# Third pair's left sums in the second chunk, spills of x in SyncE's queue, and the down projection's first two groups by half columns: one decoder layer on one Trainium2 core

## The chip, the cores and the metric

The kernel runs on one NeuronCore of a Trainium2 chip. The metric is the device time of one execution in microseconds (us); the time of a kernel is the median of several runs. A core has these engines: TensorE (PE: matmuls and transposes; its loads of the stationary operand are shown apart as PEld), VectorE (DVE), ScalarE (ACT), GpSimd (POOL) and SyncE (SP, which only issues DMAs). ACT and POOL can issue DMAs too. Every engine works through its own instructions in the order of the program; semaphores tie the engines together. Matmuls write to PSUM, eight banks of 128 x 512 float32; everything else lies in SBUF.

## The reference

One decoder layer on 256 tokens of width 2048, all float32 with random weights:

```python
h = rmsnorm(x, norm_attn_pre);  proj = h @ w_in
mixed = concat(dilated_window_attention(...), latent_attention(...))     # 8 + 8 heads
x = x + rmsnorm(mixed @ w_out, norm_attn_post)
h = rmsnorm(x, norm_mlp_pre)
u = square(relu(h @ w_up))              # 2048 -> 8192
x = x + rmsnorm(u @ w_down, norm_mlp_post)   # 8192 -> 2048
```

The change touches the second half: from the residual after `w_out` through the up projection to the first columns of the down projection.

## The kernel before

**Precision and weights.** The product of two float32 matrices is made of three matmuls of a faster type: each operand is split into a high and a low part (`hi` = the value rounded, made by ACT; `lo` = value less `hi`, made by DVE), and hi*hi, hi*lo and lo*hi are summed in PSUM (function `three`, or the loop in `down_mm`). So every weight tile of 128 x 1024 goes through four stages: a DMA into a `raw` tile (5 buffers, issued by SP at L169), `hi` on ACT (L268, or L272 where a gain is multiplied in), `lo` on DVE (L269 or L273), and the matmuls (L258). `hi` and `lo` have 8 buffers each. Class `Weights` holds a list of all weight tiles in the order of their use; `get(i)` emits the load and split of all tiles up to `i + 1 + ahead`, with `ahead` 6 (4 around the norm). Load and split of a tile are emitted together, but SP runs ahead of ACT as far as free `raw` tiles allow.

**Order of the rest.** The instructions are emitted by hand in one order per engine. A class `Flow` keeps a clock that counts the planned time of the emitted matmuls and transposes. Work beside the matmuls (evacuation of PSUM, norms, sums) is written as generators: each `yield t` says that the rest is to be emitted when the clock has advanced by `t` us; `flow.pump()` is called after each group of matmuls, `flow.finish(chain)` emits a chain to its end at once.

**Residual.** For each of the two blocks of 128 tokens, `residual(b)` updates `xs[b]` on DVE (L750, four quarters), transposes it on PE (`ht`), splits it into `hT` (hi and lo), and then writes `xs[b]` to DRAM as `xkeep[b]` with a DMA of 1 MB that ACT issues (L765); the squares for the next norm follow (L769). `x_back` reads `xkeep` near the end for the last residual. After both residuals the pools `po` and `mix` (with `xs` in it) are released, and the pool `up` takes their place.

**Up projection.** Eight chunks `j` of 1024 columns. In chunk 0 there are 16 single steps (128 rows of `w_up` each, 6 matmuls of 512 columns for each token block): the first 7 for block 0, then the same 7 for block 1, then the others for both blocks, 12 matmuls a step. From chunk 1 on, 10 single steps are left (five, then a wide one, two, a wide one, one, a wide one, two). The three wide steps take two row blocks and both token blocks at once and need 7 products instead of 8 (a scheme like Strassen's, in Winograd's form), so 21 matmuls instead of 24. They need sums of the weights (function `seven`: two loads `raw_w` of 512 KB, four DVE sums L321 to L324, four splits) and sums of the activations, which are the same for all chunks: `left_sums(kp)` for the three pairs `kp` = 0, 1, 2. These read and rewrite a part of `hT` (DVE L848 to L856, ACT L860, DVE L863) through two tiles `f` and `q`. The wide weights of chunks 1 to 6 are loaded by GpSimd (L316), those of chunk 7 through SP.

`all_sums` starts in chunk 0 at its ninth step and makes the three pairs one behind the other.

**Evacuation.** After chunk `j` each of its four accumulators is handled by a chain `up_evac`: for `j` > 0 a DVE addition (L819), then ACT's relu into a tile `r` (L822), then, D_UP = 1.8 us of the clock later, four transposes on PE (`rt`, in the accumulator's own bank), and ACT's square into `uT` (L830). `r`, and `f` and `q` of the left sums, share one tag with 2 buffers. The tiles `c` (function `close`, L881 and L883) hold sums of the wide products, and there are four tags of one buffer each.

**Down projection.** 16 groups `g` of 512 rows (4 steps `kk` of 128), two column halves `c` of 1024. `split_u(g)` splits the group's activations on ACT and DVE. The order is g outside, c inside. The accumulators of the half c = 1 lie in the banks of chunk 7's accumulators, so that before (g, c) = (0, 1) the chains of chunk 7 are finished.

Of the kernel before, what the change touches and what calls it, by code (L numbers as in the profile page):

```python
# [225 lines left out]
def layer(nc, tc, io):  # L226
# [79 lines left out]
    def seven(j, kp):  # L306


        st, tt, H = {}, nc.vector.tensor_tensor, 512

        def sums():
            for i, n in enumerate("ab"):
                src, name = up_weight(j, 2 * kp + i), f"raw_w{j}_{kp}{i}"
                if j < FF // CW - 1:
                    st[n] = late["up"].tile([P, CW], F32, tag="W", bufs=2, name=name)
                    nc.gpsimd.dma_start(out=st[n], in_=src)  # L316
                else:
                    st[n] = weights.load(src, CW, name)
            a, b = st["a"], st["b"]
            t, u = st["t"], st["u"] = [late["up"].tile([P, CW], F32, tag="T", bufs=2, name=f"{n}{j}_{kp}") for n in "tu"]  # L320
            tt(out=t[:, H:], in0=b[:, H:], in1=a[:, H:], op=OP.subtract)  # L321
            tt(out=u[:, :H], in0=t[:, H:], in1=a[:, :H], op=OP.add)
            tt(out=u[:, H:], in0=b[:, :H], in1=u[:, :H], op=OP.subtract)
            tt(out=t[:, :H], in0=a[:, H:], in1=a[:, :H], op=OP.subtract)  # L324

        def b11(hi, lo):
            split(hi[:, :H], lo[:, :H], st["a"][:, :H])

        return sums, [b11] + [lambda hi, lo, n=n: split(hi, lo, st[n]) for n in "but"]
# [4 lines left out]
    for j in range(FF // CW):  # L334
        wide_u.append([])
        for what, k in [("k", k) for k in range(KD)] if j == 0 else UP_STEPS:
# [5 lines left out]
                ts = [weights.plan(f) for f in fs]  # L342
                after = len(weights.specs)
            wide_u[j].append((what, k, ts))
    down = []
    for g in range(FF // 512):
        down.append({(c, kk): weights.plan(io["w_down"][(4 * g + kk) * P:(4 * g + kk + 1) * P, c * CW:(c + 1) * CW], 1, CW)
                     for c in range(2) for kk in range(4)})

    def in_order(n, apart=(0, 0)):  # L350

# [389 lines left out]
    def residual(b):  # L741

        po, yg, hT = late["po"], late["yg"], late["hT"]
        nc.vector.reduce_sum(ssr[b][:, 0:1], ssy[b], axis=mybir.AxisListType.X)
        r = rstd_of(ssr[b][:, 0:1], 1, D, f"post{b}", (pws[:, 0, b:b + 1], pws[:, 1, b:b + 1]))

        def update(ns):
            cs = [slice(n * 512, (n + 1) * 512) for n in ns]
            for c in cs:
                nc.vector.scalar_tensor_tensor(out=xs[b][:, c], in0=yg[b][:, c], scalar=r, in1=xs[b][:, c],  # L750
                                               op0=OP.mult, op1=OP.add)

        update((0, 1))
        yield D_NORM
        for n in range(4):
            t = tp_bank(f"ht{n}{b}")
            for k in range(4):
                transpose(t[:, k * P:(k + 1) * P], xs[b][:, n * 512 + k * P:n * 512 + (k + 1) * P])
            tv = t.rearrange("p (k s) -> p k s", k=4)
            if n in (0, 1):  # L760
                update((n + 2,))
            split(hT[0][:, 4 * n:4 * n + 4, b * P:(b + 1) * P], hT[1][:, 4 * n:4 * n + 4, b * P:(b + 1) * P], tv)
            parts[b] += 1
            yield D_HT
        nc.scalar.dma_start(out=xkeep[b], in_=xs[b])  # L765
        for n in range(4):
            c = slice(n * 512, (n + 1) * 512)
            junk = po.tile([P, 512], BF16, tag="junk", bufs=1, name=f"junkx{n}{b}")
            nc.scalar.activation(junk, xs[b][:, c], AF.Square, accum_out=ssx[b][:, n:n + 1])  # L769
            yield 0.5  # L770
        nc.vector.reduce_sum(ssr[b][:, 1:2], ssx[b], axis=mybir.AxisListType.X)
        rstd2[b] = rstd_of(ssr[b][:, 1:2], 1, D, f"pre2{b}", (1.0 / D, pws[:, 2, b:b + 1]))
        if b == NB - 1:
            weights.ahead = W_AHEAD
# [38 lines left out]

    def up_evac(j, b, i, acc, order, more=None):

        last = j >= 14
        yield (UP_STEP - 0.3 * last) * order
        if more is not None:
            nc.vector.tensor_tensor(out=acc, in0=acc, in1=more, op=OP.add)  # L819
            yield 0.9 if last else 1.6  # L820
        r = late["up"].tile([P, 512], F32, tag="r", bufs=2, name=f"r{j}_{b}")
        nc.scalar.activation(r, acc, AF.Relu, scale=rstd2[b])  # L822
        yield D_UP
        t = bank(i, f"rt{j}_{b}")
        for k in range(4):
            transpose(t[:, k * P:(k + 1) * P], r[:, k * P:(k + 1) * P])
        if j not in uT:
            tag = {"tag": "WT"[j // 2 - 6], "bufs": 2} if j >= 12 else {}
            uT[j] = late["up"].tile([P, CW], F32, name=f"uT{j}", **tag).rearrange("p (k s) -> p k s", k=4)
        nc.scalar.activation(uT[j][:, :, b * P:(b + 1) * P], t.rearrange("p (k s) -> p k s", k=4), AF.Square)  # L830
# [12 lines left out]
    def left_sums(kp):  # L843

        up, k, tt = late["up"], 2 * kp, nc.vector.tensor_tensor
        f, q = [up.tile([P, 512], F32, tag="r", bufs=2, name=f"{n}{kp}") for n in ("f", "q")]
        hs = [t[:, k:k + 2, :].rearrange("p k s -> p (k s)") for t in hT]
        tt(out=f, in0=hs[0].bitcast(F32), in1=hs[1].bitcast(F32), op=OP.add)  # L848
        for i in range(2):
            nc.vector.tensor_scalar_mul(f[:, i * S:(i + 1) * S], f[:, i * S:(i + 1) * S], gcol[:, 8 + k + i:9 + k + i])  # L850
        a11, a21, a12, a22 = [f[:, i * P:(i + 1) * P] for i in range(4)]
        s1, s2, s3, s4 = [q[:, i * P:(i + 1) * P] for i in range(4)]
        tt(out=s1, in0=a21, in1=a22, op=OP.add)
        tt(out=s2, in0=s1, in1=a11, op=OP.subtract)
        tt(out=s3, in0=a11, in1=a21, op=OP.subtract)
        tt(out=s4, in0=a12, in1=s2, op=OP.subtract)  # L856
        st = [up.tile([P, 512], F32R, name=f"st{kp}_{w}") for w in ("hi", "lo")]
        yield 3.0
        for t, x in ((hs, f), (st, q)):
            nc.scalar.activation(t[0], x, AF.Copy)  # L860
        yield 1.5
        for t, x in ((hs, f), (st, q)):
            tt(out=t[1], in0=x, in1=t[0].bitcast(F32), op=OP.subtract)  # L863
        sums.append([[t[:, i * P:(i + 1) * P] for t in st] for i in range(4)])
        yield 0.5

    def all_sums():
        for kp in range(N_SEVEN):
            yield from left_sums(kp)

    def three(out, a, w, first, last):

# [15 lines left out]
    for j in range(FF // CW):  # L888
# [9 lines left out]
        for t, b in order:  # L898
            what, k, tiles = steps[t]
            if (j, t, b) == (0, 8, 0):  # L900
                flow.finish(*res)
                late["po"].release()
                mix.release()
                late["up"] = pool("up", "right")
                s_chain = flow.start(all_sums())
            if (j, t, b) == (FF // CW - 1, 4, 0):
                weights.limit -= 1
                u_next = split_u(0)
# [40 lines left out]
    for i, (b, n) in enumerate(((0, 0), (0, 1), (1, 0), (1, 1))):  # L949
        y[b][n] = bank(i, f"y{b}{n}")  # L950
    ssd = [con.tile([P, 4], F32, name=f"ssd{b}") for b in range(NB)]
    GT = FF // 512

    def down_mm(u, g, kk, b, ns):

        wh, wl = weights.get(down[g][ns[0] // 2, kk])
        k = 4 * g + kk
        for x, ws in ((0, (wh, wl)), (1, (wh,))):
            for n in ns:
# [49 lines left out]
    hp.release()  # L1009
    dp = dpl["dp"] = pool("dp", "left")  # L1010

    for g in range(GT):
        u = u_next
        if g < GT - 1:
            for c in range(2):
                if g == 0 and c == 1:
                    flow.finish(*u_last)
                    for (b, n), to in zip(((0, 2), (0, 3), (1, 2), (1, 3)), PARTS):
                        y[b][n] = bank(at[to], f"y{b}{n}")
                for kk in range(4):  # L1020
                    for b in range(NB):
                        down_mm(u, g, kk, b, (2 * c, 2 * c + 1))
                    weights.free(down[g][c, kk])
                    flow.pump()
                    if (c, kk) == (1, 0):
                        u_next = split_u(g + 1)
            if g == 0:
                weights.limit += 1
            if g == 10:
                flow.start(x_back())  # L1030
                for n in range(4):
                    nc.sync.dma_start(out=spare(4, n), in_=io["norm_mlp_post"][:, n * 512:(n + 1) * 512]
                                      .partition_broadcast(P).rearrange("p o d -> p (o d)"))
        else:
            for c in range(2):
                for b in range(NB):
                    for n in (2 * c, 2 * c + 1):
                        for kk in range(4):
                            down_mm(u, g, kk, b, (n,))
                            flow.pump()  # L1040
                        if n < 3:
                            square(n, b)
                            gain(n, b)
                    if c:
                        fin = flow.start(final(b))
                for kk in range(4):
                    weights.free(down[g][c, kk])
    flow.finish(fin)
    up.release()
    dp.release()  # L1050
# [37 lines left out]
```

## Time and profile before

| | us |
|---|---|
| runs of the kernel before: median (lowest to highest of 3) | 1077.29 (1076.25 to 1078.84) |
| the profiled execution | 1078.73 |
| its span, first to last instruction | 1076.8 |
| PE busy in the span | 1056.5 (98%) |
| DVE busy | 701.5 (65%) |
| ACT busy | 573.7 (53%) |
| mean granted PE clock | 0.994 |

How to read it: the profile comes from one execution. An engine counts as busy while it executes; waiting, branching and issuing DMAs is not counted. Matmuls are pipelined: one of 512 columns is shown 0.39 us long, while the next one starts 0.23 us later. So busy time of PE says that PE had something in it, and what a matmul costs is read from stretches of many. "Granted clock" is the share of the full PE clock that the chip's throttle gave. In the lists of instructions a line has start, duration, engine, source line, operation, written and read tiles, shapes, count, and in brackets the idle time of the engine before it with what ended it. The rows of SP, ACTq and POOL with DMA_DIRECT2D are issues of DMAs, not transfers. The up projection's chunk 0 ends at about 402 us of the span, chunk 1 at 455, chunk 7 at 717; from there to 1065 the down projection runs.

### The profile page before, as it was taken

What the parts mean: (1) busy time and instruction counts of PE and PEld (TensorE: products, weight loads), DVE (VectorE), ACT (ScalarE), POOL (GpSimd) and SP (SyncE); (2) the same over time, 40 slices, a digit from 0 to 9 for tenths busy, and PEclk for the clock granted to TensorE, in tenths of its full rate; (3) what the DMA queues carried; (4) which work ended last, traced back from release to release, by engine and by line L of the source; (5) the groups of instructions that cost most, each with busy time, mean ns of one, the idle gap of its engine ahead of it and who ended that gap; (6) DMA issues with size and microseconds to landing.
All of it is one profiled execution on the core that took longest, in us unless ns stands there. A gap on an engine that the chain in (4) does not pass through costs nothing.

```text
span 1076.8 us, 13231 instructions
## 1 busy us (share of the span) xinstructions
PE 1056.5 (98%) x4915; PEld 878.5 (82%) x4915; DVE 701.5 (65%) x927; ACT 573.7 (53%) x763; POOL 28.1 (3%) x54
## 2 busy tenths in 40 slices
PE   9999999999999997999999999999999999999996
PEld 6888899888888776888888888787888888888885
DVE  6586546477555776879889888885444454446444
ACT  6665446565463655566655665565444444444441
POOL 0000000000000000010000000000000000000000
PEclk9999999999999998999999999999999999999999
DMA  9884546554366574646657455475665555585532
GB/s 311 303 275 142 153 123 214 150 174 161 102 236 193 177 253 137 198 156 214 219 173 232 156 192 166 157 262 185 195 194 195 194 194 193 192 311 192 194 117 78
DMA packets 74304, 206.24 MB, mean 192 GB/s; under 512 B 6912, under 2 KB 11520, under 8 KB 73856
## 3 DMA queue, kind: packets, MB, share of 16 engines
q1 hardware_dynamic: 68336, 184.06, 52.6%
q0 software_dynamic: 5184, 18.88, 5.0%
q10 hardware_dynamic: 720, 2.47, 0.7%
q8 instruction: 38, 0.62, 0.2%
q14 instruction: 26, 0.21, 0.1%
HBM read 201.18 MB, written 4.19 MB: 191 GB/s over the span
## 4 chain that ended last, share of the span: by engine, by line
PE 92%; DVE 4%; DMA 2%; issue 1%; ACT 1%; POOL 0%; DVEq 0%; POOLq 0%; ACTq 0%
PE y L258 32%; PE acc_u L258 22%; PE acc_o L258 8%; PE m L258 5%; PE acc_k L258 4%; PE acc_v L258 4%; PE acc_q L258 4%; PE acc_ckv L258 2%; PE acc_ukv L258 2%; PE acc_cq L258 2%; PE acc_uq L258 2%; DVE lo L273 1%; PE rt L262 1%; PE sc_b L258 1%; DVE lo L269 1%
## 5 line engine op out<-in xcount | busy, mean ns | idle before, releaser
L269 DVE TENSOR_TENSOR lo<-raw,hi 128x1024 fp32r<-128x1024 f32 (+3 forms) x253 | 292.8, 1165 | 244.9 <-ACT hi L268 243.1
L268 ACT ACTIVATE hi<-raw 128x1024 fp32r<-128x1024 f32 (+3 forms) x253 | 253.0, 1010 | 233.7 <-PE y L258 180.1
L258 PE MATMUL y<-hi,uhi 128*128 128x512 f32 x512 | 199.3, 389 | 0.0
L258 PE MATMUL y<-lo,uhi 128*128 128x512 f32 x512 | 199.2, 389 | 0.0
L258 PE MATMUL y<-hi,ulo 128*128 128x512 f32 x512 | 160.2, 389 | 0.0
L258 PE MATMUL acc_u<-hi,hT_hi 128*128 128x512 f32 x386 | 153.9, 399 | 0.4 <-DVE c L883 0.4
L258 PE MATMUL acc_u<-hi,hT_lo 128*128 128x512 f32 x386 | 151.1, 391 | 0.4 <-DVE hT_lo L269 0.4
L258 PE MATMUL acc_u<-lo,hT_hi 128*128 128x512 f32 x386 | 151.0, 391 | 0.0
L273 DVE SCALAR_TENSOR_TENSOR lo<-raw,gcol,hi 128x1024 fp32r<-128x1024 f32 x86 | 107.6, 1278 | 14.6 <-ACT hi L272 14.4
L272 ACT ACTIVATE hi<-raw,gcol 128x1024 fp32r<-128x1024 f32 x86 | 97.8, 1150 | 31.2 <-DMA raw<-in_w_up 13.0
L258 PEld LDWEIGHTS y<-lo,uhi 128*128 128x128 f32 x512 | 96.1, 188 | 20.0
L258 PEld LDWEIGHTS y<-hi,uhi 128*128 128x128 f32 x512 | 96.1, 188 | 20.0
L258 PEld LDWEIGHTS y<-hi,ulo 128*128 128x128 f32 x512 | 96.1, 188 | 19.9
L258 PEld LDWEIGHTS acc_u<-hi,hT_lo 128*128 128x128 f32 x386 | 72.7, 188 | 16.3 <-DVE hT_lo L269 0.8
L258 PEld LDWEIGHTS acc_u<-hi,hT_hi 128*128 128x128 f32 x386 | 72.8, 189 | 14.9 <-DVE c L883 0.8
L258 PEld LDWEIGHTS acc_u<-lo,hT_hi 128*128 128x128 f32 x386 | 72.9, 189 | 14.1
L268 ACT ACTIVATE hi<-raw_w 128x512 fp32r<-128x512 f32 (+1 forms) x42 | 35.3, 843 | 34.6 <-PE acc_u L258 29.6
L258 PE MATMUL acc_o<-hi,mixT_hi 128*128 128x512 f32 x128 | 51.8, 405 | 0.0
L258 PE MATMUL acc_o<-hi,mixT_lo 128*128 128x512 f32 x128 | 50.2, 392 | 0.0
L258 PE MATMUL acc_o<-lo,mixT_hi 128*128 128x512 f32 x128 | 50.0, 391 | 0.0
L269 DVE TENSOR_TENSOR lo<-raw_w,hi 128x512 fp32r<-128x512 f32 (+1 forms) x42 | 39.1, 954 | 13.9 <-ACT hi L268 13.5
L822 ACT ACTIVATE r<-acc_u,rstd_pre 128x512 f32<-128x512 f32 x32 | 21.8, 685 | 28.5 <-DVE acc_u L819 22.9
(247 smaller groups left out, 1514.1 us busy)
## 6 DMA issues: line engine op xcount, KB each, us to landing
raw<-in_w_down SPq DMA_DIRECT2D x128, 512.0 KB, 4.6
raw<-in_w_up SPq DMA_DIRECT2D x86, 512.0 KB, 4.4
raw<-in_w_in SPq DMA_DIRECT2D x55, 512.0 KB, 4.9
raw_w<-in_w_up POOLq DMA_DIRECT2D x36, 512.0 KB, 4.8
raw<-in_w_out SPq DMA_DIRECT2D x32, 512.0 KB, 4.4
raw<-in_w_in SPq DMA_DIRECT2D x16, 288.0 KB, 2.8
raw<-in_w_ukv SPq DMA_DIRECT2D x8, 512.0 KB, 4.9
raw<-in_w_uq SPq DMA_DIRECT2D x8, 384.0 KB, 3.3
```

Source lines behind the costliest of these rows:

```text
L258: nc.tensor.matmul(out, a, b, start=start, stop=stop)
L262: nc.tensor.transpose(out, a, ident)
L268: nc.scalar.activation(hi, src, AF.Copy)
L269: nc.vector.tensor_tensor(out=lo, in0=src, in1=hi.bitcast(F32), op=OP.subtract)
L272: nc.scalar.activation(hi, src, AF.Copy, scale=g)
L273: nc.vector.scalar_tensor_tensor(out=lo, in0=src, scalar=g, in1=hi.bitcast(F32), op0=OP.mult, op1=OP.subtract)
L822: nc.scalar.activation(r, acc, AF.Relu, scale=rstd2[b])
```

## The change

Five edits, in the diff's order:

- The two loads of the first wide pair of chunk 1 are issued by SP instead of GpSimd.
- The order of the down projection's first two groups becomes (0,0), (1,0), (0,1), (1,1) in (g, c); the weight list is planned in this order, and the split of group 1's activations is emitted after the first step. The chains of chunk 7 are finished before (0, 1) as before.
- `xkeep[b]` is written by a DMA in SP's queue instead of ACT's.
- `up_evac`: the shortened delays of the last chunk (`j >= 14`, which counts half chunks) go; for chunk 0 (`j <= 1`) the transposes are emitted 2 x D_UP instead of D_UP behind the relu.
- `left_sums`: `f` and `q` take the tags `c0` and `c1` instead of `r`; the third pair's sums are emitted 8.0 us of the clock later.

```diff
                 if j < FF // CW - 1:
                     st[n] = late["up"].tile([P, CW], F32, tag="W", bufs=2, name=name)
-                    nc.gpsimd.dma_start(out=st[n], in_=src)
+                    (nc.gpsimd if (j, kp) > (1, 0) else nc.sync).dma_start(out=st[n], in_=src)
...
-    down = []
-    for g in range(FF // 512):
-        down.append({(c, kk): weights.plan(io["w_down"][(4 * g + kk) * P:(4 * g + kk + 1) * P, c * CW:(c + 1) * CW], 1, CW)
-                     for c in range(2) for kk in range(4)})
+    GT = FF // 512
+    down, down_order = {}, [(0, 0), (1, 0), (0, 1), (1, 1)] + [(g, c) for g in range(2, GT) for c in range(2)]
+    for g, c in down_order:
+        for kk in range(4):
+            src = io["w_down"][(4 * g + kk) * P:(4 * g + kk + 1) * P, c * CW:(c + 1) * CW]
+            down[g, c, kk] = weights.plan(src, 1, CW)
...
-        nc.scalar.dma_start(out=xkeep[b], in_=xs[b])
+        nc.sync.dma_start(out=xkeep[b], in_=xs[b])
...
-        last = j >= 14
-        yield (UP_STEP - 0.3 * last) * order
+        yield UP_STEP * order
         if more is not None:
             nc.vector.tensor_tensor(out=acc, in0=acc, in1=more, op=OP.add)
-            yield 0.9 if last else 1.6
+            yield 1.6
         r = late["up"].tile([P, 512], F32, tag="r", bufs=2, name=f"r{j}_{b}")
         nc.scalar.activation(r, acc, AF.Relu, scale=rstd2[b])
-        yield D_UP
+        yield D_UP if j > 1 else 2 * D_UP
...
-        f, q = [up.tile([P, 512], F32, tag="r", bufs=2, name=f"{n}{kp}") for n in ("f", "q")]
+        f, q = [up.tile([P, 512], F32, tag=f"c{i}", bufs=1, name=f"{n}{kp}") for i, n in enumerate(("f", "q"))]
...
-        for kp in range(N_SEVEN):
+        for kp in range(N_SEVEN - 1):
             yield from left_sums(kp)
+        yield 8.0
+        yield from left_sums(N_SEVEN - 1)
...
-    for g in range(GT):
-        u = u_next
+    us = {0: u_next}
+    for g, c in down_order:
+        u = us[g]
+        if (g, c) == (0, 1):
+            flow.finish(*u_last)
+            for (b, n), to in zip(((0, 2), (0, 3), (1, 2), (1, 3)), PARTS):
+                y[b][n] = bank(at[to], f"y{b}{n}")
         if g < GT - 1:
...
+            for kk in range(4):
+                for b in range(NB):
+                    down_mm(u, g, kk, b, (2 * c, 2 * c + 1))
+                weights.free(down[g, c, kk])
+                flow.pump()
+                if kk == 0 and g + 1 not in us and (c or not g):
+                    us[g + 1] = split_u(g + 1)
```

The rest of the diff rewrites the last group's loop to the new indices without changing its order.

More of the change, by code (lines that the diff above doesn't have):

```diff
@@ L904, in layer @@
                 late["up"] = pool("up", "right")
-                s_chain = flow.start(all_sums())
+                flow.start(all_sums())
             if (j, t, b) == (FF // CW - 1, 4, 0):
@@ L951, in layer @@
     ssd = [con.tile([P, 4], F32, name=f"ssd{b}") for b in range(NB)]
-    GT = FF // 512
     def down_mm(u, g, kk, b, ns):
-        wh, wl = weights.get(down[g][ns[0] // 2, kk])
+        wh, wl = weights.get(down[g, ns[0] // 2, kk])
         k = 4 * g + kk
@@ L1010, in layer @@
     dp = dpl["dp"] = pool("dp", "left")
-    for g in range(GT):
-        u = u_next
-        if g < GT - 1:
[L1015 to L1027, printed above, removed]
+    us = {0: u_next}
[5 more added lines that the diff above has]
+                y[b][n] = bank(at[to], f"y{b}{n}")
+        if g < GT - 1:
+            for kk in range(4):
[5 more added lines that the diff above has]
+                    us[g + 1] = split_u(g + 1)
+            if (g, c) == (0, 1):
                 weights.limit += 1
-            if g == 10:
+            if (g, c) == (10, 1):
                 flow.start(x_back())
@@ L1034, in layer @@
         else:
[L1035 to L1047, printed above, removed]
+            for b in range(NB):
+                for n in (2 * c, 2 * c + 1):
+                    for kk in range(4):
+                        down_mm(u, g, kk, b, (n,))
+                        flow.pump()
+                    if n < 3:
+                        square(n, b)
+                        gain(n, b)
+                if c:
+                    fin = flow.start(final(b))
+            for kk in range(4):
+                weights.free(down[g, c, kk])
     flow.finish(fin)
```

## The prediction

> **What bounds the kernel now.** I read the page first, then PE's waits, then windows cut at the one long gap, then the timelines of ACT and DVE around it, and last SyncE's queue. The page:
>
> ```profile
> PE 1056.5 (98%) x4915; PEld 878.5 (82%) x4915; DVE 701.5 (65%) x927; ACT 573.7 (53%) x763; POOL 28.1 (3%) x54
> ...
> PE   9999999999999997999999999999999999999996
> ```
>
> TensorE (PE) is busy 98%, so time can only be won where PE stands still. Apart from both ends there is one slice below 9, the sixteenth. The windows around it (columns: stretch, length, busy us and count of PE, PEld, DVE, ACT, POOL, then granted clock, DMA share, GB/s):
>
> ```profile
> 402.58:406.20 3.62, 0.00 (x0) 0.00 (x0) 3.52 (x9) 2.72 (x4) 0.00 (x0) 1.00 0.20 81
> 406.20:410.00 3.80, 0.00 (x0) 0.00 (x0) 3.80 (x5) 0.69 (x1) 0.00 (x0) 0.50 0.39 112
> 410.00:413.05 3.05, 3.04 (x10) 2.57 (x10) 0.35 (x1) 1.89 (x3) 0.54 (x1) 0.50 0.90 262
> ...
> 455.00:498.40 43.40, 43.40 (x201) 35.94 (x200) 37.18 (x43) 27.28 (x31) 3.23 (x6) 1.00 0.59 194
> ```
>
> For 7.4 us PE does nothing, between chunk 0 and chunk 1 of the up projection. DVE is busy throughout, ACT is not. The granted clock is halved 3.6 us into the gap and still halved for 3 us after it. What ends the gap:
>
> ```profile
> 401.11 0.68 DVE L848 TENSOR_TENSOR f<-hT_hi,hT_lo 128x512 f32<-128x512 f32 x1
> ...
> 403.42 0.68 DVE L321 TENSOR_TENSOR t<-raw_w,raw_w 128x512 f32<-128x512 f32 x1
> ...
> 406.08 2.47 DVE L273 SCALAR_TENSOR_TENSOR lo<-raw,gcol,hi 128x1024 fp32r<-128x1024 f32 x2
> 408.47 0.68 DVE L863 TENSOR_TENSOR hT_lo<-f,hT_hi 128x512 fp32r<-128x512 f32 x1
> 409.07 0.68 DVE L863 TENSOR_TENSOR st_lo<-q,st_hi 128x512 fp32r<-128x512 f32 x1
> ...
> 409.27 0.69 ACT L822 ACTIVATE r<-acc_u,rstd_pre 128x512 f32<-128x512 f32 x1 [3.54 <-DVE hT_lo L863]
> ...
> 410.01 1.12 PE L262 MATMUL rt<-ident,r 128*128 128x128 f32 x4 [7.43 <-ACT r L822]
> ```
>
> PE's next instructions are transposes of `r`. `r` has two buffers under one tag, and `f` and `q` of the third pair's left sums hold both until DVE's L863 has read them; those stand behind four sums of the wide weights and two weight splits on DVE. So this is a wait for a buffer, not for weights.
>
> **Part 1: third pair's sums later, `f` and `q` in other tiles, transposes later.** Its worth, from the chain of waits and PE's timeline:
>
> ```profile
> 371.25 25.90 PE acc_u L258 x114
> ```
>
> ```profile
> 402.19 0.39 PE L258 MATMUL acc_u<-hi,hT_lo 128*128 128x512 f32 x1
> ```
>
> ```profile
> 411.12 3.02 PE acc_u L258 x9
> ...
> 460.48 0.44 PE rt L262 x4
> 460.91 2.09 PE acc_u L258 x9
> ```
>
> A matmul takes 25.90/114 = 0.227 us, so the last of chunk 0 is through at 402.42; PE starts again at 410.01: 7.59 us. At half clock four transposes take 1.12 instead of 0.44 and nine matmuls 3.02 instead of 2.09, which is 1.61 more. Together **9.20 us**. With the buffer free, what is late next? Three candidates:
>
> `r` itself. Its accumulator is complete three groups of three matmuls before the chunk's end, at 402.42 - 9 x 0.227 = 400.4. ACT then has to finish what is emitted earlier:
>
> ```profile
> 397.54 2.18 ACT L272 ACTIVATE hi<-raw,gcol 128x1024 fp32r<-128x1024 f32 x2
> 402.48 0.63 ACT L860 ACTIVATE hT_hi<-f 128x512 fp32r<-128x512 f32 x1 [2.77 <-DVE f L850]
> ...
> 404.07 1.13 ACT L272 ACTIVATE hi<-raw,gcol 128x1024 fp32r<-128x1024 f32 x1
> 405.11 0.61 ACT L268 ACTIVATE hi<-raw_w 128x512 fp32r<-128x512 f32 x1
> ```
>
> Without the two L860 of the third pair (0.63 each), ACT goes from 399.7 through 1.13 and 0.61 and starts `r` at about 401.5, done at 402.2. The transposes now stand 3.6 us of the program's clock (two times D_UP) behind it, some 404 on PE. Nothing to wait for, by 2 us.
>
> The weights.
>
> ```profile
> 398.71 1.28 DVE L273 SCALAR_TENSOR_TENSOR lo<-raw,gcol,hi 128x1024 fp32r<-128x1024 f32 x1 [0.55 <-ACT hi L272]
> ```
>
> This is the lo half of the third step of chunk 1 (steps counted along DVE's timeline). The first three steps are ready, and keep PE busy for 3 x 12 x 0.227 = 8.2 us, to 410.6 and, with the transposes, past 411. The next two (406.08, x2) are ready at 408.55 even if DVE gains nothing; without the third pair's 2.3 us ahead of 403.42 they are ready at about 406.2. Cost zero, with 5 us to spare.
>
> The third pair's sums in chunk 1. They cost DVE 403.42 - 401.11 = 2.31 and 1.20 for L863, so 3.5 us, and ACT 1.3. A full chunk has 43.40 - 37.18 = 6.2 us of DVE idle, so 41 of 43.4 us are filled, in that chunk alone. Its products are wanted only after seven single steps and two wide ones, (7 x 12 + 2 x 21) x 0.227 = 28.6 us into the chunk. Cost 0; if the idle time lies in the wrong places up to the 3.5 us. I take 0, since the same loop from 455 on shows PE busy 43.40 of 43.40 us.
>
> **Part 2: two groups of the down projection by half columns.** The last chunk's transposes have had to be done within four half-width steps; now within eight.
>
> ```profile
> 727.70:731.17 3.47, 2.18 (x18) 1.71 (x16) 0.29 (x1) 2.72 (x5) 0.00 (x0) 1.00 0.53 168
> ```
>
> ```profile
> 728.97 0.65 PE L262 MATMUL rt<-ident,r 128*128 128x128 f32 x4 [0.39 <-ACT r L822]
> 730.52 0.66 PE L262 MATMUL rt<-ident,r 128*128 128x128 f32 x4 [0.90 <-ACT r L822]
> ```
>
> Sixteen transposes at 0.44 for four would be 1.76; the stretch takes 3.47. **1.71 us** are lost to evacuation in a row; in the new order the sets fall behind the third, fourth and fifth step. The moved split of the second group's activations, a hi and a lo of 1024 columns, comes four steps earlier, after the first:
>
> ```profile
> 722.30 1.06 ACT L268 ACTIVATE hi<-raw 128x1024 fp32r<-128x1024 f32 x1 [1.66 <-PE y L258]
> ```
>
> ACT is idle 1.66 us there, enough for the 1.06 that it costs ACT. Cost 0; if it delays `r` by its full length, 1.06.
>
> **Part 3: SyncE's queue.** Two 1 MB spills and two 512 KB loads move into it, each issue at (2.72 - 0.33)/2 = 1.2 us:
>
> ```profile
> 380.45 2.72 SPq L169 DMA_DIRECT2D raw<-in_w_up  x3
> ```
>
> ```profile
> raw<-in_w_up SPq DMA_DIRECT2D x18, 512.0 KB, 4.6
> xkeep<-x ACTq DMA_DIRECT2D x2, 1024.0 KB, 4.4
> raw_w<-in_w_up POOLq DMA_DIRECT2D x2, 512.0 KB, 9.0
> ```
>
> A spill waits for the last update of its x (L750), and SyncE runs far ahead of ACT, so loads stand behind it. The program's order puts the first spill between the loads of steps 6 and 7 of chunk 0, the second between those of steps 7 and 8:
>
> ```profile
> 355.91 10.62 SPq L169 DMA_DIRECT2D raw<-in_w_up  x5
> ```
>
> ```profile
> 355.80 0.74 DVE L750 SCALAR_TENSOR_TENSOR x<-yg,rstd_post,x 128x512 f32<-128x512 f32 x1
> ...
> 367.66 0.74 DVE L750 SCALAR_TENSOR_TENSOR x<-yg,rstd_post,x 128x512 f32<-128x512 f32 x1
> ...
> 375.09 1.29 DVE L273 SCALAR_TENSOR_TENSOR lo<-raw,gcol,hi 128x1024 fp32r<-128x1024 f32 x1 [2.48 <-ACT hi L272]
> ```
>
> ```profile
> 361.56 1.14 ACT L272 ACTIVATE hi<-raw,gcol 128x1024 fp32r<-128x1024 f32 x1
> 365.13 0.60 ACT L268 ACTIVATE hT_hi<-ht 128x512 fp32r<-128x512 f32 x1 [1.06 <-PE ht L262]
> ...
> 373.92 1.14 ACT L272 ACTIVATE hi<-raw,gcol 128x1024 fp32r<-128x1024 f32 x1
> ```
>
> Step 7's load, issued long before, goes to 356.5 + 1.2 = 357.7 and lands at 362.3 (by 4.6) or 366.7 (by 9.0); ACT wants it at 361.56 and has 1.06 us to spare before hT_hi. So 0 to 4.1 us, and I take 0, from the row of its own queue. Steps 8 to 12 (the five issued from 355.91 on) go behind 368.4: step 8 issues at 369.6 and lands between 374.2 and 378.6. ACT wants it at 373.92, and PE's own need is at 402.42 - 8 x 12 x 0.227 = 380.6, which is 4.2 us after the lo that ends at 376.4. So a delay of 0.3 costs nothing and one of 4.7 costs 0.5. I take 0.
>
> ```profile
> 385.64 1.15 ACT L272 ACTIVATE hi<-raw,gcol 128x1024 fp32r<-128x1024 f32 x1 [4.24 <-DMA raw<-in_w_up]
> ```
>
> The first pair's loads leave GpSimd at 377.7 for a place behind chunk 1's third load, after 384. The loads that they slowed (ACT waits 4.24 us here) come earlier; PE does not wait there, so the gain on the path is 0. They are wanted at 403.42, and even by 9.0 us they land near 395.
>
> **The sum.** The profiled execution took 1078.73 (span 1076.8 and 1.93 around it). Less 9.20 and 1.71 it is 1067.8. The median of the runs is 1077.29, or 1.44 lower, so **1066.4**; the gain is 10.9 us, 1.0%.
>
> **The rivals.** (A) The forecast, 1066.4. By itself 1064.3 to 1068: the runs spread by 1.5 us either way, and small waits elsewhere can come or go.
>
> ```profile
> 417.63 0.68 ACT L822 ACTIVATE r<-acc_u,rstd_pre 128x512 f32<-128x512 f32 x1
> ```
>
> (B) Part of the gap stays: ACT serves the four `r` between weight splits, and a set of transposes finds its `r` late. Before, the first stood at 409.27 and the fourth here, 2.8 us apart on average, and the new places are 2.3 us of the program's clock apart. Three times 0.5 is 1.5, all of which shows if the 2 us of slack go too; with part 2 failing (1.71) it is 3.2. Against it: PE did not wait for the last three of those four. Time 1067.9 to 1069.6. The Trainium skill, page "TensorE: Matmul & The Clock Gate", Part 1, says that the clock falls to half after an idle window of about 3.4 us; by that a rest shorter than this costs only its own length, and a longer one brings the 1.61 back. The trace agrees: halved 3.6 us into the long gap, never at gaps of 0.90.
>
> (C) DVE is the bound of that stretch, not the buffer, and moving 3.5 us of it changes nothing: only part 2 is won, 1075.6, within 0.2% of before (what a measurement can just tell from no change). For it speaks DVE's full 3.80 of 3.80; against it that PE has 8.2 us of finished weights.
>
> (D) Slower: the loads of steps 8 to 12 starve PE behind the second spill. It decides from a landing at 380.6 - 2.4 = 378.2 on, and every us after that is one of PE, with 1.61 more once PE stands for over 3.6. To end 0.2% above before, PE must lose 10.9 + 2.2 = 13.1, a landing near 389.7, 20 us after its issue; it then takes 1079.5. The Trainium skill, page "DMA: Bandwidth & Descriptors", section "Anatomy of one DMA", says that DMA engines never wait for semaphores: the wait is in the issuing sequencer. By that rule all behind a spill is held until x is ready, as I assumed. In the rows the slowest landing is 9.0.
>
> **Chances.** A 0.79, B 0.14, C 0.04, D 0.03. Faster by over 0.2% are A and B, 0.93; C is within 0.2%, 0.04; slower 0.03. The range, 1064.3 to 1070.0, holds A and B.
>
> **What would show it.** Right: no PE gap over 1 us between 400 and 415 and clock 1.00 there; the wait of ACT's `r` for hT_lo gone; L863 of the third pair after chunk 0's end; no four transposes in a row near the start of the down projection. Wrong: a PE wait for DVE lo or ACT hi near 380 (D), a wait of transposes for `r` (B), a new DVE-bound wait in chunk 1 (C).

## The result, and the profile after

| | before | after |
|---|---|---|
| median (lowest to highest of 6 runs each), us | 1077.51 (1076.25 to 1078.84) | 1068.12 (1067.44 to 1068.48) |
| ratio after/before, 95% interval | | 0.9912 (0.9900 to 0.9925) |
| the profiled execution, us | 1078.73 | 1067.71 |
| its span, us | 1076.8 | 1065.5 |
| mean granted clock | 0.994 | 0.998 |

The change is worth 9.4 us. The page of after, the lines that stand against those shown of before:

```profile
PE 1054.4 (99%) x4915; PEld 876.8 (82%) x4915; DVE 701.8 (66%) x927; ACT 574.9 (54%) x763; POOL 27.2 (3%) x52
...
PE   9999999999999999999999999999999999999996
...
PEclk9999999999999999999999999999999999999999
```

The number of instructions on PE and DVE is the same; the sixteenth slice of PE is full, and no slice shows a lowered clock. PE's share of busy time went from 98% to 99% while 1% of the time was won: a share that high does not say that nothing is left. What PE waits for in after (columns: total us, times, longest):

```profile
PE warm L419 <- DVE zero L416: 1.2, 1, 1.2
PE acc_q L258 <- ACT hi L268: 1.1, 1, 1.1
PE acc_u L258 <- DVE hT_lo L269: 0.4, 1, 0.4
PE qrt L262 <- DVE qT L656: 0.2, 1, 0.2
```

There is no wait for `r` left, and none of these four lies later than chunk 0 of the up projection. Two windows of after, the boundary of chunks 0 and 1 and the whole chunk 1 (columns as in the prediction: stretch, length, busy time of PE, PEld, DVE, ACT, POOL, clock, DMA share, GB/s):

```profile
402.00:409.00 7.00, 7.00 (x36) 5.78 (x36) 6.82 (x12) 4.33 (x7) 0.75 (x1) 1.00 0.58 176
...
403.00:446.20 43.20, 43.20 (x200) 35.76 (x199) 37.83 (x47) 27.54 (x32) 3.45 (x6) 1.00 0.61 197
```

DVE is as busy at the boundary as it was before; PE now works beside it. The instructions there, from the timelines of PE, ACT and DVE (the lines of the code are 2 higher than before: L824 was L822, L850 was L848, L865 was L863):

```profile
401.18 0.69 ACT L824 ACTIVATE r<-acc_u,rstd_pre 128x512 f32<-128x512 f32 x1 [1.27 <-PE acc_u L258]
...
402.40 2.47 DVE L273 SCALAR_TENSOR_TENSOR lo<-raw,gcol,hi 128x1024 fp32r<-128x1024 f32 x2
...
402.73 0.39 PE L258 MATMUL acc_u<-hi,hT_lo 128*128 128x512 f32 x1
...
405.00 0.60 PE L262 MATMUL rt<-ident,r 128*128 128x128 f32 x4
...
405.39 0.69 DVE L850 TENSOR_TENSOR f<-hT_hi,hT_lo 128x512 f32<-128x512 f32 x1
...
411.19 0.69 DVE L865 TENSOR_TENSOR st_lo<-q,st_hi 128x512 fp32r<-128x512 f32 x1
...
436.16 0.39 PE L258 MATMUL m<-hi,hT_hi 128*128 128x512 f32 x1
```

ACT's `r` now waits for its accumulator on PE, not for DVE. The last matmul of chunk 0 starts at 402.73, chunk 1 follows without a break, the first transposes come at 405.00, 3.1 us after `r` is done. The third pair's sums begin behind the boundary, end at 411.88, and the first product that needs them (the third wide step's first `m`) starts at 436.16. The chain of waits of after, around the boundary and at the start of the down projection:

```profile
371.80 33.36 PE acc_u L258 x147
405.17 0.44 PE rt L262 x4
405.60 2.09 PE acc_u L258 x9
...
707.23 10.88 PE y L258 x48
718.11 0.87 PE rt L262 x8
...
721.73 0.44 PE rt L262 x4
...
724.93 0.44 PE rt L262 x4
```

Four transposes take 0.44 and nine matmuls 2.09, the full-clock figures. In the down projection the transposes come as 8, 4 and 4, each at 0.44 for four, with matmuls between them, where before they waited 0.39 and 0.90 us.

**Where the time came from.** The first matmul of the down projection, before and then after:

```profile
716.66 0.39 PE L258 MATMUL y<-hi,uhi 128*128 128x512 f32 x1
```

```profile
707.07 0.39 PE L258 MATMUL y<-hi,uhi 128*128 128x512 f32 x1
```

From the start of chunk 0's last matmul (402.19 before, 402.73 after) to here it is 314.47 and 304.34, so 10.13 us less. The prediction's term for the boundary is 9.20. The rest is two waits which this execution of before had late in the up projection, and after has not:

```profile
674.41 0.50 PE L258 MATMUL acc_u<-hi,hT_hi 128*128 128x512 f32 x1 [0.35 <-DVE c L883]
...
678.66 0.66 PE L262 MATMUL rt<-ident,r 128*128 128x128 f32 x4 [0.56 <-ACT r L822]
```

9.20 + 0.35 + 0.56 = 10.11. That these two waits are missing is not the work of part 1: e1_sums, which has it, shows both again (0.43 and 0.57, near 666 and 670 us). Chunk 0's end came 0.54 later, out of earlier stages that the change does not touch: its first matmul already starts 0.54 later (355.26 before, 355.80 after). The spans differ by 1076.8 - 1065.5 = 11.3, so 11.3 - 10.13 + 0.54 = 1.7 came out of the down projection, where the prediction had 1.71.

### The profile page after: what moved, and what is told of

It is laid out like the page before. It is cut to its first block, busy times and chain, and to the rows that moved or that the text cites. A ratio compares the mean times of both kernels' runs of the same rounds, so it can differ in the third digit from the quotient of the medians.

```text
span 1065.5 us, 13234 instructions
## 1 busy us (share of the span) xinstructions
PE 1054.4 (99%) x4915; PEld 876.8 (82%) x4915; DVE 701.8 (66%) x927; ACT 574.9 (54%) x763; POOL 27.2 (3%) x52
## 4 chain that ended last, share of the span: by engine, by line
PE 96%; DVE 1%; issue 1%; DMA 1%; ACT 0%; POOL 0%; DVEq 0%; POOLq 0%; ACTq 0%
PE y L258 32%; PE acc_u L258 25%; PE acc_o L258 8%; PE m L258 5%; PE acc_k L258 4%; PE acc_v L258 4%; PE acc_q L258 4%; PE acc_ckv L258 2%; PE acc_ukv L258 2%; PE acc_cq L258 2%; PE acc_uq L258 2%; PE rt L262 1%; PE sc_b L258 1%; PE sc_a L258 0%; PE o_a L258 0%
## 5 line engine op out<-in xcount | busy, mean ns | idle before, releaser
L273 DVE SCALAR_TENSOR_TENSOR lo<-raw,gcol,hi 128x1024 fp32r<-128x1024 f32 x86 | 107.7, 1280 | 11.5 <-ACT hi L272 11.3
L824 ACT ACTIVATE r<-acc_u,rstd_pre 128x512 f32<-128x512 f32 x32 | 21.9, 687 | 26.1 <-DVE acc_u L821 22.7
```

Of the source, the lines that this page charges most:

```text
L273: nc.vector.scalar_tensor_tensor(out=lo, in0=src, scalar=g, in1=hi.bitcast(F32), op0=OP.mult, op1=OP.subtract)
```

## The experiments

The theory T is the prediction's: the loss at the boundary is a wait for the two buffers of `r`, with the half clock that follows from it; the down order is worth its 1.7; the queue is worth nothing. Against it stand Q, that the new queue costs something which hides a larger gain elsewhere, and V, that DVE's work is the bound there and the tags alone do little. All medians in one table (us; the kernel before was run again beside each set of four):

| run | what it is | median (lowest to highest) | before beside it | ratio (95%) |
|---|---|---|---|---|
| e1_sums | part 1 alone | 1069.30 (1068.22 to 1070.03) | 1077.42 | 0.9922 (0.9908 to 0.9936) |
| e2_down | part 2 alone | 1075.59 (1074.48 to 1077.31) | 1077.42 | 0.9981 (0.9972 to 0.9990) |
| e3_queue | part 3 alone | 1076.87 (1075.72 to 1079.21) | 1077.42 | 0.9994 (0.9985 to 1.0003) |
| e4_before_again | before | 1077.62 (1076.55 to 1079.06) | 1077.42 | 1.0000 (0.9991 to 1.0009) |
| e5_tag | only the new tags of `f`, `q` | 1071.96 (1070.36 to 1072.66) | 1077.55 | 0.9940 (0.9927 to 0.9952) |
| e7_keep_busy | before, gap filled with matmuls | 1076.17 (1075.02 to 1077.47) | 1077.55 | 0.9986 (0.9977 to 0.9995) |
| e8_no_queue | parts 1 and 2 | 1067.04 (1066.81 to 1068.24) | 1077.55 | 0.9901 (0.9887 to 0.9914) |
| e9_spill3 | after, two more copies behind the spill | 1071.84 (1071.56 to 1073.22) | 1077.55 | 0.9947 (0.9935 to 0.9960) |
| e10_dup1 | after, with D_UP once | 1067.08 (1066.73 to 1067.68) | 1077.45 | 0.9906 (0.9890 to 0.9923) |
| e11_after_again | after | 1067.39 (1067.13 to 1067.72) | 1077.45 | 0.9909 (0.9895 to 0.9924) |
| e12_loads_only | after, spills on ACT as before | 1066.86 (1065.89 to 1067.07) | 1077.45 | 0.9902 (0.9888 to 0.9917) |
| e13_no_queue_again | parts 1 and 2 | 1067.12 (1066.47 to 1067.60) | 1077.45 | 0.9906 (0.9891 to 0.9921) |

**Part 1 alone (e1_sums).** On the kernel before:

```diff
-        yield D_UP
+        yield D_UP if j > 1 else 2 * D_UP
...
-        f, q = [up.tile([P, 512], F32, tag="r", bufs=2, name=f"{n}{kp}") for n in ("f", "q")]
+        f, q = [up.tile([P, 512], F32, tag=f"c{i}", bufs=1, name=f"{n}{kp}") for i, n in enumerate(("f", "q"))]
...
-        for kp in range(N_SEVEN):
+        for kp in range(N_SEVEN - 1):
             yield from left_sums(kp)
+        yield 8.0
+        yield from left_sums(N_SEVEN - 1)
```

> Part 1 alone (f and q under the tags c0 and c1, the third pair 8.0 us later, 2 x D_UP in chunk 0; the down projection and the queues as before). Theory T (the terms of the sum add up; the shortfall of the median is only the profiled execution of before, which lost more than its fellows): 7.7 to 9.2 us below the median of before, the long gap gone and the clock 1.00 behind it. Theory Q (SyncE's queue costs about 1.5 us that the sum left out): the full 9.2 us or more, since the queue is not touched here. Theory V (DVE was the bound of the gap): within 2 us of before.

Measured: 8.1 us won, inside T's 7.7 to 9.2 and short of Q's. The gap at the boundary is gone, and the two waits at the start of the down projection are there as before:

```profile
720.25 0.66 PE L262 MATMUL rt<-ident,r 128*128 128x128 f32 x4 [0.39 <-ACT r L822]
721.81 0.66 PE L262 MATMUL rt<-ident,r 128*128 128x128 f32 x4 [0.90 <-ACT r L822]
```

The boundary is the sums' affair alone, and neither the queue nor the down order has a part in it.

**Part 2 alone (e2_down).** The diff's hunks on `down` and `down_order`, and `up_evac` without the shortened delays of the last chunk; nothing else:

```diff
-        last = j >= 14
-        yield (UP_STEP - 0.3 * last) * order
+        yield UP_STEP * order
...
-    for g in range(GT):
-        u = u_next
+    us = {0: u_next}
+    for g, c in down_order:
+        u = us[g]
```

> Part 2 alone (order of the first two groups of the down projection, longer delays in the last chunk's chains). T and Q: 1.7 us below before, no waits of transposes for r near 728 us; the long gap at 402 us stays. If the new order hides nothing: 0.

Measured: 1.8 us won (0.1 to 0.28%), against 1.71 in the prediction. The gap stayed:

```profile
408.53 1.12 PE L262 MATMUL rt<-ident,r 128*128 128x128 f32 x4 [5.67 <-ACT r L824]
```

It is 5.67 here, 1.76 shorter than in the prediction's profile, although nothing of this kernel ahead of the last chunk's evacuation is changed but the code lines. That is a first sign that the gap's length varies from one execution to the next.

**Part 3 alone (e3_queue).**

```diff
-                    nc.gpsimd.dma_start(out=st[n], in_=src)
+                    (nc.gpsimd if (j, kp) > (1, 0) else nc.sync).dma_start(out=st[n], in_=src)
...
-        nc.scalar.dma_start(out=xkeep[b], in_=xs[b])
+        nc.sync.dma_start(out=xkeep[b], in_=xs[b])
```

> Part 3 alone (both spills and the first pair's loads in SyncE's queue). T: within 1 us of before, the gap at 402 us stays 7 us long or becomes some us shorter, as DVE gets the loads earlier. Q: 1 to 2 us slower than before, with PE waits that before does not have. Theory D of the prediction: PE starves near 380 us, over 2 us slower.

Measured: 0.55 us, with an interval that includes no change, so that Q's 1 to 2 us and rival D's loss are not there. The gap is:

```profile
408.47 1.11 PE L262 MATMUL rt<-ident,r 128*128 128x128 f32 x4 [5.78 <-ACT r L822]
```

**Before once more (e4_before_again).** The kernel unchanged, for a second profile.

> The kernel before, unchanged, profiled once more. T: this execution loses less than the first profiled one: the stretch at half clock after the gap is shorter than 3.05 us or the two waits near 674 us (0.35 and 0.56) are gone; its time lies nearer 1077. Q: the same waits as in the first profile, and the time differs only by noise that no wait shows.

Measured: the same median, and in the profiled execution (1077.88) a shorter gap than in the first profile, with no wait near 674:

```profile
409.95 1.12 PE L262 MATMUL rt<-ident,r 128*128 128x128 f32 x4 [6.72 <-ACT r L822]
```

What goes with the gap's length is how long ACT waited for a weight load near 385 us, after the norm. The prediction quotes 4.24 us for its profile, whose gap is 7.43. In e4:

```profile
385.58 1.15 ACT L272 ACTIVATE hi<-raw,gcol 128x1024 fp32r<-128x1024 f32 x1 [3.62 <-DMA raw<-in_w_up]
```

in e2, and in e3:

```profile
384.17 1.15 ACT L272 ACTIVATE hi<-raw,gcol 128x1024 fp32r<-128x1024 f32 x1 [2.72 <-DMA raw<-in_w_up]
```

```profile
381.59 4.93 ACT L272 ACTIVATE hi<-raw,gcol 128x1024 fp32r<-128x1024 f32 x4 [1.67 <-DMA raw<-in_w_up]
```

A wait of 4.24 goes with a gap of 7.43, 3.62 with 6.72, 2.72 with 5.67, 1.67 with 5.78; the last pair is out of order. A late load makes DVE's weight splits late, the third pair's L863 stands behind them, and `r` behind L863. The start of that L863 (L865 in e2) follows the waits in all four, 408.47, 408.40, 407.00 and 406.93 us; the gap does not, because chunk 0's end, from which it counts, lies at 402.58, 403.23, 402.86 and 402.69. The order of the instructions makes this cause likely; four executions do not prove it.

**Only the tags (e5_tag).** Third pair where it was, D_UP as it was:

```diff
-        f, q = [up.tile([P, 512], F32, tag="r", bufs=2, name=f"{n}{kp}") for n in ("f", "q")]
+        f, q = [up.tile([P, 512], F32, tag=f"c{i}", bufs=1, name=f"{n}{kp}") for i, n in enumerate(("f", "q"))]
```

> Only the tags of f and q change against before (c0 and c1 instead of r); the third pair stays in chunk 0 and the transposes stay 1.8 us of the clock behind the relu. Theory B1 (the buffer was the whole wait): the gap at 402 us falls below 3.4 us, no half clock, 6 to 9 us below before. Theory B2 (the buffer hid a second wait: ACT still has the third pair's L860 and two splits ahead of r, which DVE feeds late): r starts at 405.7 to 406 instead of 409.3, a gap of about 4 us is left and with it the half clock; 3 to 4 us below before.

Measured: 5.6 us won by one line; V would have it near nothing. What is left at the boundary, from PE's and ACT's timelines (the profiled execution, 1070.36, is the fastest of the five, 1.6 under their median, so these rows do not show what the slower ones lose):

```profile
401.45 0.63 ACT L860 ACTIVATE st_hi<-q 128x512 fp32r<-128x512 f32 x1 [0.42 <-DVE q L856]
401.99 1.13 ACT L272 ACTIVATE hi<-raw,gcol 128x1024 fp32r<-128x1024 f32 x1
403.03 0.61 ACT L268 ACTIVATE hi<-raw_w 128x512 fp32r<-128x512 f32 x1
403.55 0.66 ACT L822 ACTIVATE r<-acc_u,rstd_pre 128x512 f32<-128x512 f32 x1
...
404.26 0.66 PE L262 MATMUL rt<-ident,r 128*128 128x128 f32 x4 [1.93 <-ACT r L822]
```

`r` does not wait for its buffer any more. It stands on ACT behind the two L860 of the third pair (the second is shown), which themselves wait for DVE, and behind two weight splits. This is the second wait that lay under the first one. B2 had named it, but too large: `r` starts at 403.55 and not at 405.7 to 406, and the gap of 1.93 leaves the clock at 1.00 (the windows 400.00 to 404.30 and 404.30 to 412.00 both have it), as B1 had it. The gain lies between the two forecasts. Part 1 as a whole (e1_sums, 2.5 us better against its own before) takes the second wait away, by the later sums: the later transposes turn out not to be needed (e10_dup1). The other half, later sums with `f` and `q` still under the tag of `r`, wasn't tried.

**The gap filled (e7_keep_busy).** On the kernel before, ahead of the first block's transposes, 30 matmuls into a bank that nobody reads:

```diff
+        if (j, b) == (0, 0):
+            keep = bank(7, "keep_busy")
+            for _ in range(30):
+                nc.tensor.matmul(keep, tok(hT[0], 8, 0), hT[0][:, 8:10, :].rearrange("p k s -> p (k s)"), start=True, stop=True)
```

> Before, with 30 more matmuls of 512 columns on PE ahead of the first transposes of chunk 0, written to a bank that nobody reads (6.8 us of work inside the gap; the output is unchanged). It prices the half clock alone. Theory H (the clock falls only because PE stands still): clock 1.00 throughout, 1 to 2 us below before. If the half clock belongs to something else at that place: no change in time and the clock still 0.50 for 6.8 us. If r comes before the 30 matmuls are through, the gain shrinks by what is left of them.

Measured: 1.4 us won (0.05 to 0.23%) by adding work. `r` is as late as ever, and PE is merely kept warm until it comes; the window from the last real matmul to the first transpose:

```profile
402.48:409.43 6.95, 6.95 (x31) 5.45 (x30) 6.88 (x12) 2.93 (x5) 0.00 (x0) 1.00 0.26 76
```

The clock is at 1.00 there, and stays so in the stretch behind it, so the 1.4 comes from the clock alone. It is rather a lower bound of the half clock's price, which the prediction had at 1.61: the 30 matmuls take 6.8 us, and in an execution whose gap would be shorter (5.67 in e2) they hold PE up themselves.

**Parts 1 and 2 without the queue (e8_no_queue, e13_no_queue_again).** After, with part 3's two edits undone (the diff of e3_queue, backwards).

> The changed kernel without part 3: spills on ACT and the first pair's loads on GpSimd as before, parts 1 and 2 as changed. Prediction's view: the same as the changed kernel within 1 us, since no PE wait hangs on these loads; ACT waits of 4 us for raw loads near 385 us come back. Rival: the queue part is needed once the gap is gone, because DVE then lacks the time that the two early loads take from the others; 1 us or more slower than the changed kernel, with a PE wait for a lo half in the first steps of chunk 1.

> Parts 1 and 2 without part 3, once more, now beside the changed kernel on one chip. If part 3 costs about 1 us, as the medians of two different calls (1067.0 against 1068.1) say: 1 us below the changed kernel again. If that was the call: the same within 0.5 us.

Measured: 1067.04, then 1067.12 beside an after of 1067.39. The first, 1.1 under the 1068.12 of after, looked like a price of part 3; run beside after it is 0.3 with overlapping ranges. The difference lay between the sets of runs. In e8's profile ACT waits again for a load of the stretch that part 3 had relieved:

```profile
384.52 1.15 ACT L272 ACTIVATE hi<-raw,gcol 128x1024 fp32r<-128x1024 f32 x1 [2.63 <-DMA raw<-in_w_up]
```

and PE waits for none of it: with the boundary mended, nothing on the path depends on that load. Part 3 wins nothing; whether it costs a few tenths is taken up with e12 below.

**More behind the spill (e9_spill3).** After, with two more copies of 1 MB to DRAM that nobody reads, behind the second spill:

```diff
+        if b == 1:
+            for i in range(2):
+                nc.sync.dma_start(out=dram.tile([P, D], F32, name=f"xmore{i}"), in_=xs[b])
```

> The changed kernel with two more copies of the second spill (1 MB each, to DRAM that nobody reads) behind it in SyncE's queue, ahead of the loads of steps 8 to 12. It tests rival D's price. If a DMA of 1 MB holds the queue for 2.5 us, the load of step 8 lands 5 us later than 375.3, its lo is ready near 382.8, PE needs it at 381.2: 1.5 to 2 us slower than the changed kernel, as a PE wait for DVE lo near 381 us. If queues share the engines so that a later load overtakes: no loss.

Measured: about 4 us slower than after. First after's own queue, issues of SP and then ACT's use of step 8:

```profile
357.54 0.38 SPq L169 DMA_DIRECT2D raw<-in_w_up  x1
368.98 0.33 SPq L768 DMA_DIRECT2D xkeep<-x  x1
369.40 16.42 SPq L169 DMA_DIRECT2D raw<-in_w_up  x11
...
385.87 0.90 SPq L316 DMA_DIRECT2D raw_w<-in_w_up  x2
...
375.31 1.15 ACT L272 ACTIVATE hi<-raw,gcol 128x1024 fp32r<-128x1024 f32 x1 [0.75 <-DMA raw<-in_w_up]
```

And the same of e9, with PE's waits:

```profile
369.61 1.39 SPq L771 DMA_DIRECT2D xmore<-x  x2
371.09 19.88 SPq L169 DMA_DIRECT2D raw<-in_w_up  x11
...
380.47 1.15 ACT L272 ACTIVATE hi<-raw,gcol 128x1024 fp32r<-128x1024 f32 x1 [5.66 <-DMA raw<-in_w_up]
...
382.99 0.50 PE L258 MATMUL acc_u<-lo,hT_hi 128*128 128x512 f32 x1 [0.82 <-DVE lo L273]
...
415.64 0.66 PE L262 MATMUL rt<-ident,r 128*128 128x128 f32 x4 [1.19 <-ACT r L827]
...
450.20 0.47 PE L258 MATMUL acc_u<-hi,hT_hi 128*128 128x512 f32 x1 [0.53 <-DVE c L890]
451.50 0.50 PE L258 MATMUL acc_u<-hi,hT_hi 128*128 128x512 f32 x1 [0.36 <-DVE c L890]
```

Step 8 is issued 1.7 us later and its split starts 5.16 later: 3.5 us of that are not the issue's delay, and the two megabytes on their way at the same time are the likely cause. PE stands at step 8 for 0.82 by the row, about 1.1 counted from start to start of its matmuls. Then ACT and DVE run late into chunk 1: the fourth set of transposes there waits 1.19 for its `r`, and at the chunk's end PE waits twice for DVE's `c`. Counted from chunk 0's first matmul (355.80 in after, 356.06 in e9), e9 is 1.5 us behind at the first transposes (405.00 and 406.72), 2.9 at the first product of a wide step (418.48 and 421.63) and 4.0 at the down projection's start (707.07 and 711.35). The expected 1.5 to 2 us are those of step 8; the rest came in chunk 1. So the rival D has a real mechanism, and two megabytes more are enough to set it off.

**Is 2 x D_UP needed (e10_dup1)?** After, with `yield D_UP` alone.

> The changed kernel with D_UP instead of 2 x D_UP ahead of chunk 0's transposes. Theory S (the later place gives 2 us of slack that the r tiles need): PE waits for r again, 1 us or more in sum over the four sets, up to 1.5 us slower than the changed kernel. Rival (r is early enough once the third pair is out of the way): no PE wait over 0.3 us, same time.

Measured: 1067.08 beside an after of 1067.39, and no wait for `r` on PE. The second `r` is done and its transposes come, in ACT's and PE's timelines:

```profile
403.61 0.68 ACT L824 ACTIVATE r<-acc_u,rstd_pre 128x512 f32<-128x512 f32 x1
...
405.00 0.60 PE L262 MATMUL rt<-ident,r 128*128 128x128 f32 x4
```

0.7 us are left. The doubled delay is reserve, not gain.

**After once more, and its loads alone (e11_after_again, e12_loads_only).** The first is after unchanged; the second puts the two spills back into ACT's queue:

```diff
-        nc.sync.dma_start(out=xkeep[b], in_=xs[b])
+        nc.scalar.dma_start(out=xkeep[b], in_=xs[b])
```

> The changed kernel unchanged, on the chip of the three others. Theory T (with the long gap gone, the run-to-run spread of before goes too): median 1067.5 to 1068.5, highest less lowest under 1.6 us against 2.6 to 3.4 for before.

> The changed kernel with the spills back on ACT; only the first pair's loads stay with SyncE. If the spills in SyncE's queue cost something (step 8 of chunk 0 has its lo 3.4 us ahead of PE instead of 4.3): up to 1 us faster than the changed kernel. If not: same within 0.6 us.

Measured: after 1067.39, 10.1 under its before and 0.1 under the 1067.5 to 1068.5 expected, with its runs 0.6 apart. e12 is 0.5 lower still, the lowest median of all. Its interval overlaps after's nearly whole, but both intervals carry the spread of before; run against run, all four of e12 lie below all four of after. The profiles point the same way: from chunk 0's first matmul to the down projection's first it is 351.27, 351.48 and 351.51 us where the spills are in SP's queue (after, e11, e10), and 350.94, 350.96 and 351.11 where they are in ACT's (e8, e12, e13). So moving the spills probably cost some 0.4 us, 0.04%. Apart from one of 0.23 in e11 no wait on PE shows where, and four runs of each do not settle it.

## Why the prediction was right, point by point

- **The cause at the boundary: right.** It is the buffers of `r`. One line that gives `f` and `q` other tiles won 5.6 us with DVE's work unchanged (e5_tag), so V and the prediction's rival C fall.
- **The size of part 1: right for its profile.** 9.20 worked out; 10.13 measured over the stretch, of which 0.91 are two waits named above that other executions of before lack. Alone it won 8.1 on the medians (e1_sums), 1.1 less than the term.
- **The half clock's 1.61 as a part of it: right.** 1.4 at least when taken away by itself (e7_keep_busy).
- **"With the buffer free, what is late next?": right that nothing is.** `r` started at 401.18 (predicted 401.5), though by another last wait: the prediction let ACT's splits set it, and in after ACT had been idle for 1.27 us and waited for the accumulator. The next two `lo` were ready at 404.9 (406.2), the third pair's sums cost PE nothing, with 24 us to spare. (The 28.6 us to the first product that needs them counted seven single steps; there are eight, and it came 33.2 us after chunk 0's end.) DVE in chunk 1 is busy 37.83 us of 43.2, where the prediction worked out 41 of 43.4: there was even more room. A late `r` behind ACT's splits, as in rival B, is what e5_tag shows for the first `r` and e9_spill3 for the fourth. The measured time lies within B's 1067.9 to 1069.6, but not by B's mechanism: in after PE waits for no `r`.
- **Part 2: right.** 1.71 predicted, 1.7 in the profile, 1.8 alone on the medians. The sets of transposes fell behind the fourth, fifth and sixth step (48, 12 and 12 matmuls of 12 a step), not the third, fourth and fifth; the sum does not depend on it.
- **Part 3 at nothing: right within some 0.4 us.** Step 7's load (landing predicted for 362.3) came later than ACT wanted it: its split began at 363.20, after 1.00 us of waiting, which the 1.06 to spare took up. Step 8's split began at 375.31 behind a landing predicted for 374.2 to 378.6. The wide weights were issued at 385.87 (after 384). What the spills may cost is shown with e12.
- **Rival D's price: too low.** The prediction counted one us of PE for each us of landing after 378.2. In e9 the split began at 380.47, so 2.3 by that count; up to the first transposes 1.5 were lost, less than that, but the run lost 4 in all, because the lateness came up again in chunk 1. The Trainium skill, page "DMA: Bandwidth & Descriptors", section "Anatomy of one DMA", says that the engines of a DMA do not wait for semaphores and that any such wait is the issuing engine's, so that what stands behind a spill is held by its issuer; the rows of after's queue agree, since SP issues nothing between the load at 357.54 and the spill at 368.98.

- **The step that failed: "or 1.44 lower".** The sum for the profiled execution came to 1067.8, and the profiled execution of after took 1067.71. That it fits so well is in part luck: after also lacks the two waits of 0.91, which the sum left in, and loses as much again by a chunk 0 that starts 0.54 later and by 0.28 more outside the span (2.21 against 1.93). The prediction then took off 1.44, because the first profile of before was that much above the median, as if the excess were spread over the program and would come back in after. It was not. This execution had a gap of 7.43 where e4, e3 and e2, which have the same sums and tags, had 6.72, 5.78 and 5.67: 1.0 more than the mean of the four, 6.40, and 1.4 more than that of the other three. So 1.0 to 1.4 us of the excess lay in the very wait that the change removes and were counted twice, once in the 9.20 and once in the 1.44. The two waits of 0.91 belong to the excess too, but not to the 9.20. The whole stretch says the same: from chunk 0's first matmul to the down projection's first, the first profile of before takes 361.40 us, e4 359.73, e3 359.04 and e2 358.66, against 351.27 and 351.48 in the two profiles of after. The 9.20 is the size of one long gap, and other executions have less to win there. The forecast, 1066.4, is 1.7 below the 1068.12 measured first and 1.0 below the 1067.39 measured later; both are in the range of 1064.3 to 1070.0.

What stays open: why the loads near 385 us land at different times in different executions, whether that alone sets the gap's length, what makes the waits near 674 come and go (the first profile and e1_sums have them, e4, e3 and e2 do not), and where the spills in SP's queue lose their few tenths, if they do.

## What to carry to other kernels

Where a wait for a buffer ends an idle stretch, look at who else shares the buffer's tag: a tile name in a helper off the path can cost the path 5 us, and one line can tell. Then ask what is second in the queue, since here a second wait, 1.93 in the one profile of it, lay under the first. And if the term that an edit removes varies from execution to execution, price it from more than one profile, or forecast from the profiled execution without correcting to the median afterwards.

## What the runs showed of the hardware that was not expected

**The clock can fall less than 3 us after the last matmul.** In e4 the half clock begins 3.9 us after the last matmul and lasts 6.8 us; in e2 it begins between 405.6 and 405.7, less than 3 us after chunk 0's last matmul, which ends at 402.86 (windows of e4, then of e2; the number behind POOL's is the clock):

```profile
403.23:407.15 3.92, 0.00 (x0) 0.00 (x0) 3.85 (x7) 2.19 (x3) 0.00 (x0) 1.00 0.02 9
407.15:413.97 6.82, 4.02 (x12) 3.35 (x13) 3.86 (x6) 2.81 (x4) 0.54 (x1) 0.50 0.72 231
```

```profile
402.86:405.60 2.74, 0.00 (x0) 0.00 (x0) 2.71 (x4) 1.39 (x2) 0.00 (x0) 1.00 0.00 0
...
405.70:412.50 6.80, 3.97 (x12) 3.29 (x13) 3.84 (x6) 2.81 (x4) 0.54 (x1) 0.50 0.72 223
```

The Trainium skill, page "TensorE: Matmul & The Clock Gate", Part 1, says that windows of about 3.4 us run freely and that the clock is halved after at least one idle window. The length of the half clock, 6.8 in both, is two such windows, which fits. A start 2.8 us after the last matmul can't follow a window that was idle throughout, so by these rows a window with some work at its beginning must count as idle, or the windows are shorter than the page has them. So the prediction's border, a rest of 3.4 to 3.6 us that costs only its own length, is not a safe one. The gap of 1.93 in e5_tag kept the full clock; for gaps between 1.93 and 5.67 these runs do not say what they cost beyond their own length.

**An evener kernel.** In one set of runs, after's four lie within 0.6 us and before's seven within 2.0. That fits a gap whose length varies and that after does not have. Against it, the four of e1_sums lie 1.8 apart, and that kernel does not have the gap either; nothing here settles it.
